# GpSimd multiplies the probabilities of the second and third attention with their reciprocals, and the weave's step lengths follow

## The chip, the cores and the metric

The kernel runs on one core of one Trainium2 chip. What is measured is the device time of one execution in microseconds (us); lower is better. The engines are TensorE (PE, its weight loads PEld), VectorE (DVE), ScalarE (ACT), GpSimd (POOL) and SyncE (SP, which issues most DMAs).

## What is computed

One layer of a decoder trunk on 1024 tokens of width 1024, in float32. One input projection feeds three token mixers: differential attention with 4 heads (A), sliding-window attention with 8 heads, 2 key groups, a window of 128 and sinks (B), and a sparse attention with 8 heads and 2 key groups that adds three branches, compressed, selected and window 512 (C). Their outputs are projected, gated and merged, and an MLP with squared ReLU follows. What the change touches is the normalization in B and C:

```python
# B: softmax over the band with a sink in the denominator
e = jnp.exp(s - m)
p = e / (jnp.sum(e, axis=-1, keepdims=True) + jnp.exp(sk - m))
o = jnp.einsum('bngrqk,bnkgd->bnqgrd', p, vb)
# C: three softmaxes, each weighted by its gate
out = g[..., 0:1] * o_cmp + g[..., 1:2] * o_sel + g[..., 2:3] * o_win
```

With 16 selected blocks of 64 and 1024 tokens, the selected branch sees every causal key.

## The kernel before

Float32 products are split into a high and a low part, and one product is three matmuls, `mm3` (L118 to L120). The split (`split`, L90 and L91) takes an ACT copy for the high part and a subtraction on DVE or POOL for the low one.

Each attention is a sequence of *items*: a pair of 128-query tiles for one head (C, 16 items per key group) or two heads (B, 8 items per key group). An item has *rows* and *groups*. A row issues the logits of one 128-query tile (L711), a minimum on DVE (signs are turned, so it is the maximum; L721, L725, L727, L728, L735, and L1097 for the compressed keys), the exponential with its sum on ACT (L743), and then what the change touches: DVE adds up the sums (L936 to L938 in B, L1042 in C), takes reciprocals (L939; L1043, multiplied by the gates in L1044), and multiplies the probabilities in place: L941 in B (`p`, two heads of up to 256 columns), L1046 in C (`pc`, the 64 compressed columns, then `p` with up to 1024 selected and up to 640 window columns). A group transposes up to four 128x128 blocks of probabilities on PE (L759), splits them out of PSUM into `ph` (ACT, L90) and `pl` (DVE, L91), after POOL zeroed the blocks that are not visible (L756, L757), and later multiplies them with the values into one accumulator (L901, L902). At the end of a head ACT and DVE empty that accumulator (L907, L908); there is one such accumulator, three buffers for logits and two for transposes.

`pipeline` (L670) runs the rows of one item between the groups of the item before it. `step` (L695) emits one group: value products of an earlier group, then the transposes of this one. Each row and step gives two numbers, its PE time and its DVE time as the code estimates them, in us; the second is `d`. `mix` (L155) is the weave: it puts dense work (projections, gates, the first branch product) between these fine steps, as far as the estimated DVE time demands, and what is left over runs behind the last fine step:

```python
for pe, dve in fine:
    now += pe
    goal = max(goal + pace * dve, now - SLACK)
    while step is not None and now < goal and (self.through or ahead < AHEAD):
        now += step
        ahead += 1
        step = next(dense, None)
while step is not None:
    step = next(dense, None)
```

`PACE` (L67) holds the factors: 1.4144 and 1.156 for the two key groups of B, 1.392 and 1.45 for those of C. The dense work is, in B, 64 steps of `project_b` (0.495 each) for the first key group and 32 steps of two gate columns (0.65 each) for the second. In C it is 192 steps of 12 gate columns (`gates`, L1102) for the first key group and `first_branch` (L1148) for the second: 16 and 64 gate steps, 8 branch steps of 2.6 each, then 32 and 16 gate steps and 8 more branch steps. A gate column loads two 128x512 weights, splits them (ACT L90, POOL L91), and stores two results. A branch step loads a weight and a stored gate, runs 12 matmuls, multiplies on DVE (L1162) and stores. Ahead of each key group of C stands `project_c`, which runs alone. `merge_and_mlp` follows C.

PE's order is the order of the program text, so it is this weave. The other engines' order is set when the kernel is built, by a simulated schedule with priorities; each engine then works through its own queue in order.

Of the kernel before, what the change touches and what calls it, by code (L numbers as in the profile page):

```python
# [14 lines left out]
ALU = mybir.AluOpType  # L15
# [60 lines left out]
class Kernel:  # L76
# [835 lines left out]
    def items_b(self, g, sta):  # L912
        nc, at = self.nc, self.at
        bias = self.bias
        for qb, r0 in [(qb, r0) for qb in range(4) for r0 in (0, 2)]:
            pq = [None, None]
            hs = slice(4 * g + r0, 4 * g + r0 + 2)

            def row(j, qb=qb, r0=r0, hs=hs, pq=pq):
                t = 2 * qb + j  # L920
                n = min(2, t + 1) * P
                ps = self.sc()
                p = at.tile([P, 2, 256], F32, name="p", tag=f"p{r0 // 2}", bufs=2)
                l = at.tile([P, 3, 2], F32, name="lb", tag="lb", bufs=4)
                m = at.tile([P, 2], F32, name="mb", tag="mb", bufs=4)
                k0 = max(t - 1, 0)
                d = 0.0
                for i in range(2):
                    self.logits(ps, i * 256, t, sta["logits"][r0 + i], k0 * P, k0 * P + 256)
                for i in range(2):  # L930
                    x = ps[:, i * 256:i * 256 + n]
                    h = 4 * g + r0 + i
                    d += self.near_min(m[:, i:i + 1], x, bias[:, r0 + i, :], self.sink[:, 1, h:h + 1])
                    self.expo(p[:, i, 0:n], x, m[:, i:i + 1], l[:, 0, i:i + 1])

                nc.vector.tensor_tensor(l[:, 1, :], self.sink[:, 0, hs], m, op=ALU.add)  # L936
                nc.scalar.activation(l[:, 1, :], l[:, 1, :], AF.Exp)
                nc.vector.tensor_tensor(l[:, 1, :], l[:, 1, :], l[:, 0, :], op=ALU.add)  # L938
                nc.vector.reciprocal(l[:, 2, :], l[:, 1, :])  # L939
                for i in range(2):  # L940
                    nc.vector.tensor_scalar(p[:, i, 0:n], p[:, i, 0:n], l[:, 2, i:i + 1], None, op0=ALU.mult)  # L941
                pq[j] = (p, k0)
                return 0.43, d + 0.65

            rows = [lambda j=j, row=row: row(j) for j in range(2)]
            groups = []
            kts = list(range(max(2 * qb - 1, 0), 2 * qb + 2))
            box = {}
            for i in range(2):
                def prow(j, kt, i=i, pq=pq):  # L950
                    p, k0 = pq[j]
                    return p[:, i, (kt - k0) * P:(kt - k0 + 1) * P]

                r = r0 + i
                dst = self.od[4 + 2 * g + r // 2, (r % 2) * 64:(r % 2) * 64 + 64, qb * 256:(qb + 1) * 256]
                for grp in ([kts] if len(kts) == 2 else [kts[0:1], kts[1:3]]):
                    def values(i, ph, pl, grp=grp, kts=kts, box=box, dst=dst):
                        kt = grp[i]
                        return self.head_values(box, dst, sta["v"][:, kt, :], ph, pl, kt == kts[0], kt == kts[-1])

                    groups.append(self.group(prow, qb, grp, lambda t, kt: t - 1 <= kt <= t, values))
            yield dict(rows=rows, groups=groups, end=[])

    def items_c(self, g, sta):
        nc, at = self.nc, self.at
        bias4 = self.bias
        for r in range(4):
            for qb in range(4):
# [51 lines left out]
                def win_near(j, mem, qb=qb, r=r, bias=bias, hd=hd, rows=rows):  # L1020
                    t = 2 * qb + j
                    n = (t + 1) * P
                    l, m = mem["l"], mem["m"][:, 2, :]
                    k0 = 0 if t < 4 else t - 1
                    w = n - k0 * P
                    ps = self.sc()
                    cost = self.logits(ps, 0, t, sta["win"][r], k0 * P, k0 * P + max(w, 256))
                    nw = min(w, 256)
                    d, init = 0.0, m[:, 1:2] if k0 else None
                    if w > nw:  # L1030
                        d += self.far_min(m, 1, ps[:, 0:w - nw])
                        init = m[:, 1:2]
                    d += self.near_min(m, ps[:, w - nw:w], bias, 3e38 if init is None else init)
                    p = self.prob(qb, 640, "w")
                    f = 384 if k0 else 0
                    if f:
                        self.expo(p[:, 0:f], mem["wf"], m[:, 0:1], l[:, 1, 1:2])
                    self.expo(p[:, f:f + w], ps[:, 0:w], m[:, 0:1], l[:, 0, 2:3])
                    nw = f + w
                    if "sf" in mem:  # L1040
                        e = 2 if f else 1
                        nc.vector.tensor_tensor(l[:, 0, 1:1 + e], l[:, 0, 1:1 + e], l[:, 1, 0:e], op=ALU.add)  # L1042
                    nc.vector.reciprocal(l[:, 1, 0:3], l[:, 0, 0:3])  # L1043
                    nc.vector.tensor_tensor(l[:, 1, 0:3], l[:, 1, 0:3], self.cgate[:, t, 3 * hd:3 * hd + 3], op=ALU.mult)  # L1044
                    for x, k, i in ((mem["c"], 64, 0), (mem["s"], n, 1), (p, nw, 2)):
                        nc.vector.tensor_scalar(x[:, 0:k], x[:, 0:k], l[:, 1, i:i + 1], None, op0=ALU.mult)  # L1046
                    rows[j] = (mem["c"], mem["s"], p, max(t - 4, 0))
                    return cost, d + 0.55 + 0.52e-3 * (n + nw)

                steps = []  # L1050
                for j in range(2):
# [537 lines left out]
```

## Time and profile before

| | |
|---|---|
| three runs | 2040.56, 2041.63, 2045.64 us, median 2041.63 |
| the profiled execution | 2045.69 us, span 2043.7 us |
| busy over the span | PE 1901.7, PEld 1621.5, DVE 1423.4, ACT 1022.0, POOL 954.3 us |
| second attention | 410 to 562 us of the span |
| third attention, first key group | 612 to 862 us |
| third attention, second key group | 918 to 1196 us |
| granted TensorE clock, mean | 0.980 |

The span runs from the first to the last instruction; the time has some 2 us more around it. A busy time is the union of an engine's instructions. A row of instruction groups names the line, the engine, the operation, what it writes and reads with the shape, how many there were, then their busy time in us, the mean of one in ns, and the idle time in front of them with what ended it. A row of waits reads: who waited, for whom, how long in total, how many times, the longest.

### The profile page before, as it was taken

What the parts mean: (1) busy time and instruction counts of PE and PEld (TensorE: products, weight loads), DVE (VectorE), ACT (ScalarE), POOL (GpSimd) and SP (SyncE); (2) the same over time, 40 slices, a digit from 0 to 9 for tenths busy, and PEclk for the clock granted to TensorE, in tenths of its full rate; (3) what the DMA queues carried; (4) which work ended last, traced back from release to release, by engine and by line L of the source; (5) the groups of instructions that cost most, each with busy time, mean ns of one, the idle gap of its engine ahead of it and who ended that gap; (6) DMA issues with size and microseconds to landing.
All of it is one profiled execution on the core that took longest, in us unless ns stands there. A gap on an engine that the chain in (4) does not pass through costs nothing. (4 is left out here: it accounts for less than half of the span.)

```text
span 2043.7 us, 30701 instructions
## 1 busy us (share of the span) xinstructions
PE 1901.7 (93%) x9838; PEld 1621.5 (79%) x9838; DVE 1423.4 (70%) x3231; ACT 1022.0 (50%) x2626; POOL 954.3 (47%) x1142
## 2 busy tenths in 40 slices
PE   7999888988799999999999899999899998999998
PEld 6888887888688888887888677787688886888876
DVE  6757777788848677648676755657755544889898
ACT  5456556666636555536555533335455544444331
POOL 4455355544352212162222227218444445789784
PEclk9999999999999999999999899999899998999999
DMA  5131022011211111212242456425444446355343
GB/s 218 51 104 52 4 55 59 26 38 37 87 28 61 56 52 51 72 33 91 68 147 77 159 198 204 147 93 161 172 167 160 144 145 247 119 167 163 124 144 114
DMA packets 122558, 219.49 MB, mean 107 GB/s; under 512 B 14420, under 2 KB 35412, under 8 KB 122396
## 3 DMA queue, kind: packets, MB, share of 16 engines
q1 hardware_dynamic: 120812, 211.75, 31.9%
q10 hardware_dynamic: 1584, 5.77, 0.9%
q8 instruction: 78, 1.28, 0.3%
q14 instruction: 84, 0.69, 0.1%
HBM read 156.59 MB, written 64.81 MB: 108 GB/s over the span
## 5 line engine op out<-in xcount | busy, mean ns | idle before, releaser
L91 POOL TENSOR_TENSOR wl<-wr,wh 128x512 fp32r<-128x512 f32 (+3 forms) x246 | 328.8, 1343 | 275.0 <-ACT wh L90 238.8
L90 ACT ACTIVATE wh<-wr 128x512 fp32r<-128x512 f32 (+3 forms) x258 | 150.3, 590 | 183.8 <-PE mm L119 124.1
L711 PE MATMUL sc<-st 128*128 128x256 f32 (+5 forms) x736 | 183.9, 344 | 25.9 <-ACT p L743 25.3
L90 ACT ACTIVATE ph<-tr 128x384 fp32r<-128x384 f32 (+3 forms) x280 | 138.4, 497 | 105.5 <-PE tr L759 87.0
L91 DVE TENSOR_TENSOR pl<-tr,ph 128x384 fp32r<-128x384 f32 (+3 forms) x280 | 155.8, 559 | 40.2 <-ACT ph L90 37.6
L756 POOL MEMSET ph<- 128x128 f32 x152 | 35.7, 235 | 291.3 <-PE ac L901 253.0
L711 PEld LDWEIGHTS sc<-st 128*128 128x128 f32 x736 | 122.8, 192 | 47.5 <-ACT p L743 38.8
L118 PE MATMUL mm<-hh,wh 128*128 128x512 f32 x384 | 158.8, 414 | 0.0
L120 PE MATMUL mm<-hh,wl 128*128 128x512 f32 x384 | 151.5, 395 | 0.0
L119 PE MATMUL mm<-hl,wh 128*128 128x512 f32 x384 | 151.4, 394 | 0.0
L119 PE MATMUL mm<-wl,wh 128*128 128x512 f32 x352 | 139.5, 396 | 9.4 <-POOL wl L91 9.4
L118 PE MATMUL mm<-wh 128*128 128x512 f32 x352 | 139.9, 398 | 8.2 <-DVE x L1471 5.3
L90 ACT ACTIVATE wh<-u 128x512 fp32r<-128x512 f32 x162 | 93.0, 620 | 106.3 <-PE mm L119 27.9
L759 PE MATMUL tr<-ident,p 128*128 128x128 f32 x792 | 129.2, 275 | 16.9 <-ACT o L889 7.8
L120 PE MATMUL mm<-wh,wl 128*128 128x512 f32 x352 | 139.1, 395 | 0.0
L743 ACT ACTIVATE p<-sc,mc 128x256 f32<-128x256 f32 (+5 forms) x200 | 106.7, 538 | 52.0 <-DVE mc L735 47.0
L901 PE MATMUL ac<-ph,st 128*128 128x256 f32 x392 | 109.8, 298 | 19.4 <-DVE ob L908 11.5
L91 POOL TENSOR_TENSOR wl<-s,wh 128x512 fp32r<-128x512 f32 x64 | 89.5, 1405 | 79.3 <-ACT wh L90 79.3
L118 PE MATMUL mm<-wh,hh 128*128 128x384 f32 (+1 forms) x320 | 117.0, 366 | 0.0
L91 DVE TENSOR_TENSOR wl<-u,wh 128x512 fp32r<-128x512 f32 x98 | 112.5, 1150 | 3.9 <-ACT wh L90 3.9
L902 PE MATMUL ac<-pl,st 128*128 128x256 f32 x392 | 106.5, 292 | 6.5 <-DVE pl L91 5.8
L91 POOL TENSOR_TENSOR wl<-u,wh 128x512 fp32r<-128x512 f32 x64 | 98.8, 1557 | 25.1 <-ACT wh L90 25.0
(311 smaller groups left out, 5771.2 us busy)
## 6 DMA issues: line engine op xcount, KB each, us to landing
ud<-u SPq DMA_DIRECT2D x112, 256.0 KB, 2.2
u<-ud SPq DMA_DIRECT2D x98, 256.0 KB, 3.3
wr<-wu SPq DMA_DIRECT2D x76, 256.0 KB, 2.8
wr<-wd SPq DMA_DIRECT2D x64, 256.0 KB, 2.9
gd<-go SPq DMA_DIRECT2D x48, 256.0 KB, 2.0
g<-gd SPq DMA_DIRECT2D x48, 256.0 KB, 3.2
wr<-wg SPq DMA_DIRECT2D x40, 256.0 KB, 2.7
wr<-wbr SPq DMA_DIRECT2D x40, 256.0 KB, 3.0
```

The costliest lines, as they stand in the source:

```text
L90: nc.scalar.activation(hi, src, AF.Copy)
L91: (eng or nc.vector).tensor_tensor(lo, src, hi.bitcast(F32), op=ALU.subtract)
L118: mm(out, lh, rh, start=first, stop=False, skip_group_check=more)
L119: mm(out, lh, rl, start=False, stop=False, skip_group_check=more)
L120: mm(out, ll, rh, start=False, stop=last, skip_group_check=more)
L711: self.nc.tensor.matmul(ps[:, off:off + k1 - k0], q[:, t * P:(t + 1) * P], k[:, k0:k1], start=i == 0, stop=i == 1)
L743: self.nc.scalar.activation(p, ps, AF.Exp, bias=m, scale=-1.0, accum_out=l)
L756: nc.gpsimd.memset(ph[0:rows, o:o + P].bitcast(F32), 0.0)
L759: nc.tensor.transpose(pt[0:rows, o:o + P], src, self.ident)
L901: nc.tensor.matmul(ac, v, ph, start=first, stop=False)
L902: nc.tensor.matmul(ac, v, pl, start=False, stop=last)
```

## The change

The multiplications of L941 and L1046 move from DVE to POOL, with the same operands, and the estimates `d` that those rows hand to the weave become smaller: in B by 0.25 per row (16 rows per key group), in C by 0.52e-3 us for each selected and window column of the row (`n + nw`). `PACE` stays as it is.

```diff
                 nc.vector.tensor_tensor(l[:, 1, :], l[:, 1, :], l[:, 0, :], op=ALU.add)
                 nc.vector.reciprocal(l[:, 2, :], l[:, 1, :])
                 for i in range(2):
-                    nc.vector.tensor_scalar(p[:, i, 0:n], p[:, i, 0:n], l[:, 2, i:i + 1], None, op0=ALU.mult)
+                    nc.gpsimd.tensor_scalar(p[:, i, 0:n], p[:, i, 0:n], l[:, 2, i:i + 1], None, op0=ALU.mult)
                 pq[j] = (p, k0)
-                return 0.43, d + 0.65
+                return 0.43, d + 0.4
...
                     for x, k, i in ((mem["c"], 64, 0), (mem["s"], n, 1), (p, nw, 2)):
-                        nc.vector.tensor_scalar(x[:, 0:k], x[:, 0:k], l[:, 1, i:i + 1], None, op0=ALU.mult)
+                        nc.gpsimd.tensor_scalar(x[:, 0:k], x[:, 0:k], l[:, 1, i:i + 1], None, op0=ALU.mult)
                     rows[j] = (mem["c"], mem["s"], p, max(t - 4, 0))
-                    return cost, d + 0.55 + 0.52e-3 * (n + nw)
+                    return cost, d + 0.55
```

## The prediction

> **What bounds the kernel now.** I read the page's first part, then the stretches in which the edited lines run, then the waits that end in them. Over the whole span TensorE is busy 93%:
>
> ```profile
> PE 1901.7 (93%) x9838; PEld 1621.5 (79%) x9838; DVE 1423.4 (70%) x3231; ACT 1022.0 (50%) x2626; POOL 954.3 (47%) x1142
> ```
>
> The windows view cuts the edited part into stages. Columns: stretch, its length, busy time of PE, PEld, DVE, ACT, POOL, granted clock, DMA share, GB/s.
>
> ```profile
> 410.00:484.00 74.00, 65.01 (x426) 61.08 (x425) 60.26 (x204) 47.44 (x171) 35.98 (x88) 0.95 0.11 30
> 484.00:562.00 78.00, 63.98 (x397) 55.52 (x396) 65.94 (x235) 51.80 (x172) 26.67 (x91) 0.97 0.26 75
> ...
> 612.00:862.00 250.00, 240.70 (x1399) 207.96 (x1398) 182.12 (x603) 147.49 (x427) 55.73 (x109) 1.00 0.18 59
> ...
> 918.00:1118.00 200.00, 191.30 (x1101) 165.05 (x1101) 149.96 (x484) 118.72 (x341) 49.14 (x89) 1.00 0.30 92
> 1118.00:1196.00 78.00, 62.98 (x332) 52.21 (x331) 55.02 (x156) 40.60 (x107) 19.70 (x35) 0.91 0.40 129
> ```
>
> 410 to 562 is the second attention (two key groups), 612 to 862 and 918 to 1196 are the two groups of the third; between them PE runs projections alone. Length minus PE busy is what can be won: 9.0, 14.0, 9.3, 8.7 and 15.0 us, 56.0 in all. The last stretch also lost 0.09 x 78 = 7.0 us to the clock (0.91). So PE's fixed list of work sets the time, DVE is close behind in the second attention (60.26 of 74, 65.94 of 78), and the loss per microsecond is largest from 1118 on. What PE waits for there, and first in the second attention:
>
> ```profile
> PE sc L711 <- ACT p L743: 9.1, 7, 3.2
> PE tr L759 <- DVE pc L1046: 1.8, 1, 1.8
> ```
>
> ```profile
> PE ac L901 <- DVE ob L908: 11.5, 11, 2.0
> ```
>
> The logits wait until ScalarE has read the previous ones, which wait for minima on DVE; the first value product of a head waits until DVE has emptied the only accumulator. Both are DVE latency, bare where no dense matmul stands between. Counting the dense ones alone (first of their three lines) shows why the ends are bad: 6 in the last 24 us of the second attention, 1 in the last 29 of the third.
>
> ```profile
> 538.00:562.00 24.00, 2.57 (x6) 1.42 (x6) 0.90 0.26 78
> ...
> 1167.00:1196.00 29.00, 0.71 (x1) 0.20 (x1) 0.99 0.11 33
> ```
>
> **The change, part by part: DVE.** It loses these groups (columns: busy us, mean ns, idle before):
>
> ```profile
> L1046 DVE TENSOR_SCALAR p<-p,lc 128x640 f32<-128x640 f32 (+7 forms) x128 | 67.8, 571 | 0.0
> ...
> L941 DVE TENSOR_SCALAR p<-p,lb 128x256 f32<-128x256 f32 (+1 forms) x64 | 24.8, 425 | 0.5
> L1046 DVE TENSOR_SCALAR pc<-pc,lc 128x64 f32<-128x64 f32 x64 | 22.2, 346 | 1.7
> L1044 DVE TENSOR_TENSOR lc<-lc,cgate 128x3 f32<-128x3 f32 x64 | 12.8, 200 | 2.0
> ```
>
> That is 24.8 us of 126.2 in the second attention and 67.8 + 22.2 = 90.0 of 387.1 in the third. L1044, which stays, is used below.
>
> **POOL.** It gains 192 + 64 instructions. No multiply by a per-partition scalar ran there, so I bound it:
>
> ```profile
> L91 POOL TENSOR_TENSOR wl<-wr,wh 128x512 fp32r<-128x512 f32 x180 | 258.8, 1441 | 252.6 <-ACT wh L90 233.3 <-DVE lc L1044 15.2 <-PE mm L119 2.4
> ...
> L91 POOL TENSOR_TENSOR st<-raw,st 128x128 fp32r<-128x128 f32 x48 | 23.3, 488 | 22.9 <-ACT st L90 22.9
> ...
> masks.py:199 POOL TENSOR_SCALAR_AFFINE_SELECT ident<-ident 128x128 f32<-128x128 f32 x1 | 0.3, 292 | 0.1
> ```
>
> The two-input rows give (1441 - 488) / 384 = 2.48 ns an element over 171 ns; the one single-input row is 292 ns at 128. The code's sizes add up to 15,360 elements a partition for L941 and 71,680 for L1046 (a head: 64 x 8, selected 4608, window 3840). Upper end, as two inputs: 64 x 0.171 + 38.1 = 49 us and 192 x 0.171 + 177.8 = 211 us. Lower end: what DVE needed, 24.8 and 90.0. I take half the two-input slope through the 292 ns row (133 ns + 1.24 an element), since that row is the nearest in kind: 27.6 and 114 us. POOL is now busy 62.7 us of 152 and 124.6 of 528, so even the upper end leaves it at 73% and 63%: no throughput bound.
>
> **The new waits.** A multiply on POOL waits for L939 or L1044 on DVE, and the transposes of the next item wait for it. Behind it in POOL's queue stand weight residues (L91) and the zeroing of ph and pl; ahead of it can stand a zeroing that itself waits for PE:
>
> ```profile
> POOL ph L756 <- PE ac L901: 101.6, 28, 12.2
> ```
>
> So far that was idle POOL and free (918 to 1196). One row of the third attention, DVE, then POOL, then the transposes that need it:
>
> ```profile
> 707.91 0.16 DVE L1044 TENSOR_TENSOR lc<-lc,cgate 128x3 f32<-128x3 f32 x1
> 708.11 1.30 DVE L1046 TENSOR_SCALAR pc<-pc,lc 128x64 f32<-128x64 f32 x1
> ```
>
> ```profile
> 708.08 1.29 POOL L91 TENSOR_TENSOR wl<-wr,wh 128x512 fp32r<-128x512 f32 x1 [5.99 <-DVE lc L1044]
> ```
>
> ```profile
> 712.68 0.38 PE L759 MATMUL tr<-ident,pc 128*128 128x128 f32 x2
> ```
>
> The multiply ended at 709.41, 3.27 us before its use. On POOL, behind the same 1.29 us residue, it would end near 709.37 + 0.21: hidden, also at 0.33 (upper end). Of all these multiplies one made PE wait, the 1.8 us of the waits quoted above; I add that and nearly as much again for late rows, 3 us. The ends: 0, and a mean multiply (114 / 192 = 0.6 us) in each of 32 items, 19 us.
>
> The same rows show DVE and POOL blocking each other: the 64-element multiply took 1.30 us beside a residue against a mean of 346 ns. That contention leaves with the edit, but L1044 and its like (two inputs from SBUF) have it too: 0.16 us alone, 200 ns on average, with POOL at 24% of the third attention. At (124.6 + 114) / 528 = 45% I take another 0.04 us on each such instruction (L728 56, L1042 40, L1044 64, L936 and L938 32 each: 224): 9 us, so DVE still sheds 106. Upper bound, each meeting a multiply as often as POOL is busy and waiting out its whole mean of 0.6 us: 224 x 0.45 x 0.6 = 60 us.
>
> The Trainium skill (SBUF — State Buffer, "Who interferes with whom") states that a VectorE instruction with two SBUF inputs contends with a GpSimd one that reads SBUF, and that the later one blocks fully; by that rule the edit swaps one blocked instruction for another, and the sum would be that of the second rival below. The 1.30 us row agrees in kind.
>
> **The weave.** `mix` puts dense steps in until pace x the sum of the figures d is reached. The code's figures for one group of the third attention sum to 159.9 over 194 fine steps; the edit takes 0.52e-3 x 8448 x 4 = 17.6 off. First group: 1.392 x 159.9 - 99.8 (its own PE figures) = 122.8 of 124.8 dense before; 1.392 x 142.3 - 99.8 = 98.3 after, so about 40 of 192 steps are pushed behind the last fine one. Second group, also 124.8 of dense work: 1.45 x 159.9 - 99.8 = 132.1 used it up 18 fine steps early (the empty 29 us); 1.45 x 142.3 - 99.8 = 106.6 reaches the end and leaves 6 branch steps of 2.6 behind it. Second attention (0.25 x 16 = 4.0 off 41.3 and off 44.0): in its first half 1.4144 x 37.3 - 25.9 = 26.9 of 31.7, so 9 of 64 steps stay behind; in its second, stepped through by the same rule, the last dense step moves from the 39th fine step to the 50th of 50. What these weigh on PE:
>
> ```profile
> 1118.17 0.39 PE L118 MATMUL mm<-xh,wh 128*128 128x512 f32 x1
> ...
> 1118.86 0.39 PE L118 MATMUL mm<-xh,wh 128*128 128x512 f32 x1
> ...
> 1120.89 0.28 PE L901 MATMUL ac<-ph,st 128*128 128x256 f32 x1
> ```
>
> A dense step is 0.69 us, a branch step 2.72; so 27.6 + 16.3 + 9 x 0.53 = 48.7 us of dense work leaves the fine stretches and runs alone behind them. That costs nothing if those stretches, 96% PE in the third attention, get as much shorter. Each of the 6 branch steps takes along its weight load, its gate load and its store (256 KB each) on SP's queue, one ScalarE and one POOL split and one DVE product; the merge's loads stand behind them on SP, under 16.3 us of PE work. I price that at 0; at worst PE waits for its first two loads, some 5 us.
>
> **The sum**, against this execution's 2045.69 us. 410 to 484: 9.0 lost, DVE a fifth lighter but thinner cover, -2. 484 to 562: 14.0 lost, the end now covered, -5. First group, -2 of 9.3, second to 1118, -1 of 8.7: PE-bound already. From 1118: 22.0 lost with the clock; the 56 us of work would lose 2.5 at the rate of the stretch before; I credit half of the 19.5 between, since coarse steps and a bare drain of the last item remain, -10. Late rows +3. Sum -17, 2028.7. The median of the runs is 4.06 us below this execution, so 2024.6, said as 2025.
>
> **Rivals.** *The fine stretches don't get shorter* (the other side). They may be held by the chain minimum, exponential, sum, multiply, transpose, and not by PE's list; ScalarE is at 59% in the first group and would rise to 66%. Then the 48.7 us run on top. The place is 612 to 862; it decides where more than 17 / 48.7 = 35% is not made up. For it: PE waits for ACT p and DVE ob are latency; against: 240.70 of 250 busy. At 60% kept on top: 2024.6 + 29 = 2054.
>
> *The port eats it.* With the 60 us bound DVE sheds 55 of 115, the gains of 20 halve, and late rows stay: -10 + 3 gives 2035; with the 19 us of late rows instead of 3, 2051. For it: the 1.30 us row; against: L1044's mean of 200 ns beside a POOL at 24%.
>
> *DVE was the bound in the second attention after all*, and the end of the third closes well: 14 of the 23.0 us there, 19 of 22.0 from 1118, 4 in between, no late row: 2041.6 - 37 = 2005.
>
> *The edit is hidden*: PE's list stays the bound and its few gaps keep their length, 2042.
>
> **How the numbers follow.** Forecast 0.42 (own range 2014 to 2033), DVE-bound 0.16, port with the nearer price 0.08 and with the further 0.06, hidden 0.06, stretches don't shorten 0.22. Within 0.3% (6.1 us, about what a measurement here tells from no change) is 2035.5 to 2047.8: hidden 0.06, half of the nearer port 0.04, and edges of the neighbours 0.06, together 0.16. Faster: 0.42 + 0.16 + 0.04, less 0.03 for the forecast's edge, 0.59. Slower: 0.22 + 0.06 less 0.03, 0.25. The range reaches to the outer cases, 2005 to 2056.
>
> **What the profile after would show.** No L941 or L1046 on DVE, 256 multiplies on POOL of 28 and 114 us; DVE some 100 us lighter. Dense steps until the end of each attention, some 28 us of gates alone after the first group and 16 us of branch steps after the second. PE's idle share in the last 80 us before the merge falls from 19% to below 12%. Wrong would make me: transposes L759 waiting for POOL L1046, L1042 or L728 above 400 ns, a first group whose fine stretch stays near 250 us, or multiplies above 2 us.

## The result, and the profile after

The changed kernel is slower. Its median is 2061.3 us (five runs, 2053.0 to 2065.9) against 2040.56 us before on the same chip (2039.7 to 2045.6), a ratio of 1.0087 with a 95% interval of 1.0064 to 1.0110. The interval is about 9 us wide, and the medians differ by 20.7 us where that ratio makes 18; differences below are between medians, so a few us of them mean little. The forecast was 2025, its range 2005 to 2056: even the range missed. The profiled execution took 2065.94 us, its span is 2064.2 us and its mean clock 0.972, where the one before had 2045.69, 2043.7 and 0.980; both are some 5 us above their medians.

The first part of the page after:

```profile
PE 1909.1 (92%) x9838; PEld 1628.0 (79%) x9838; DVE 1343.6 (65%) x2975; ACT 1022.4 (50%) x2626; POOL 1226.0 (59%) x1398
```

DVE is 79.8 us lighter (1423.4 before), POOL 271.7 us heavier (954.3). PE issues as many matmuls as before and is busy 7.4 us longer, at a lower mean granted clock. The windows of the kernel after, cut where its own stages end (columns as in the prediction):

```profile
406.00:484.00 78.00, 70.64 (x475) 65.87 (x474) 57.04 (x198) 54.07 (x194) 64.05 (x127) 0.98 0.15 42
484.00:561.00 77.00, 64.82 (x365) 56.54 (x365) 53.42 (x182) 47.42 (x155) 53.55 (x119) 0.87 0.22 65
608.00:854.00 246.00, 228.80 (x1339) 199.09 (x1338) 151.69 (x516) 145.09 (x425) 159.92 (x207) 0.97 0.16 51
854.00:878.00 24.00, 24.00 (x107) 19.87 (x106) 2.13 (x3) 4.89 (x9) 4.93 (x4) 1.00 0.28 91
878.00:933.00 55.00, 51.89 (x234) 40.78 (x232) 19.39 (x37) 17.94 (x47) 30.85 (x43) 0.94 0.14 38
933.00:1160.00 227.00, 212.94 (x1236) 183.87 (x1235) 151.04 (x500) 140.84 (x409) 154.12 (x193) 0.99 0.25 82
1160.00:1199.00 39.00, 31.82 (x161) 26.53 (x160) 21.28 (x42) 20.27 (x43) 25.23 (x29) 0.82 0.64 191
1199.00:1221.00 22.00, 11.82 (x51) 9.52 (x50) 4.84 (x8) 2.19 (x5) 1.29 (x1) 0.83 0.81 280
```

Four things stand in these rows. The fine stretch of the third attention's first group (third row) lost dense work and yet has more idle PE: 246.00 - 228.80 = 17.2 us against 10.2 before (258.00 - 247.78, in the windows of the kernel before under e11). The gates pulled out of it run alone at 100% (fourth row). `project_c` for the second group (fifth row) takes 54.5 us by its first and last matmul where it took 47.2. And in the last row, the branch steps behind the last fine step, PE works 11.8 of 22 us. Measured by the first and last matmul of each stage, the 20.5 us between the two spans are: -1.9 up to the end of the first `project_c` (1.4 of it by 384 us, ahead of any edited line), +11.8 in the first group with its gates alone, +7.3 in the second `project_c`, +7.7 in the second group with its branch steps alone, and -4.4 from the merge on.

The groups of POOL in the kernel after, shapes apart, from 400 to 1222 us:

```profile
L1046 POOL TENSOR_SCALAR p<-p,lc 128x640 f32<-128x640 f32 x40 | 75.4, 1889 | 0.0
L941 POOL TENSOR_SCALAR p<-p,lb 128x256 f32<-128x256 f32 x56 | 52.0, 941 | 10.6 <-DVE lb L939 5.7 <-ACT ph L90 3.5 <-ACT st L562 1.2
L1046 POOL TENSOR_SCALAR pc<-pc,lc 128x64 f32<-128x64 f32 x64 | 29.8, 466 | 84.2 <-DVE lc L1044 75.5 <-ACT ph L90 4.3 <-PE sc L711 1.8
...
L1046 POOL TENSOR_SCALAR p<-p,lc 128x1024 f32<-128x1024 f32 x8 | 22.8, 2848 | 0.0
```

From 640 to 1024 columns the time grows by 959 ns: 2.50 ns an element over some 0.29 us. The idle column tells the order: POOL stands idle 84.2 us ahead of the first multiply of a row (`pc`), 75.5 of it for L1044, and not at all ahead of the other two. The three come as one burst. What PE waits for in the same stretch:

```profile
PE ac L901 <- DVE ob L908: 15.6, 18, 3.0
PE ac L901 <- POOL ph L756: 12.8, 9, 3.7
PE mm L118 <- DVE g L1162: 10.2, 1, 10.2
...
PE tr L759 <- POOL p L1046: 1.5, 4, 0.6
PE ac L901 <- POOL pl L757: 1.2, 1, 1.2
```

The second row is new. The transposes hardly wait for the multiplies (fourth row shown); the value products wait for the *zeroing* of `ph`, a memset of 0.2 us that stands behind the multiplies in POOL's queue. One such case in the timeline of the kernel after:

```profile
834.67 0.16 DVE L1044 TENSOR_TENSOR lc<-lc,cgate 128x3 f32<-128x3 f32 x1
...
835.00 0.45 POOL L1046 TENSOR_SCALAR pc<-pc,lc 128x64 f32<-128x64 f32 x1 [2.08 <-DVE lc L1044]
...
835.42 4.71 POOL L1046 TENSOR_SCALAR p<-p,lc 128x1024 f32<-128x1024 f32 x2
...
835.79 0.28 PE L901 MATMUL ac<-ph,st 128*128 128x256 f32 x1
...
840.07 0.21 POOL L756 MEMSET ph<- 128x128 f32 x1
...
840.33 0.58 PE L901 MATMUL ac<-ph,st 128*128 128x256 f32 x1 [3.69 <-POOL ph L756]
```

POOL waits 2.08 us for the reciprocals, then works 5.1 us through a row whose probabilities PE needs later, and only then zeroes the block that PE needs now. PE is idle 3.69 us and comes back at half clock: this matmul takes 0.58 us, its like 0.28 before the gap.

The 10.2 us wait stands at the end of the branch steps. DVE in the timeline of the kernel after:

```profile
1204.76 0.69 DVE L1162 SCALAR_TENSOR_TENSOR g<-g,mm 128x512 f32<-128x512 f32 x1 [1.48 <-DMA g<-gd]
1212.13 0.69 DVE L1162 SCALAR_TENSOR_TENSOR g<-g,mm 128x512 f32<-128x512 f32 x1 [6.68 <-DMA y<-yd]
1219.29 0.69 DVE L1162 SCALAR_TENSOR_TENSOR g<-g,mm 128x512 f32<-128x512 f32 x1 [3.23 <-DMA g<-gd]
```

And PE in the same timeline, at the end of its last branch step and the start of the merge:

```profile
1209.56 0.39 PE L120 MATMUL mm<-xh,wl 128*128 128x512 f32 x1
1220.12 0.76 PE L118 MATMUL mm<-ob,wh 128*128 128x512 f32 x1 [10.18 <-DVE g L1162]
```

PE is done with the branch steps at 1209.9, but their last products with the gates come 7 us apart: a gate is loaded into one of two buffers, multiplied in place and stored from it, and only then can the next load start, behind the merge's loads on SP. The result of a branch step stays in PSUM until its product has read it, and the merge's first matmul waits for the last of these products: the 10.18 us. With fine steps between the branch steps this ring had time; alone, at 2.7 us of PE work each, they do not.

### The profile page after: what moved, and what is told of

It reads as the page before. It is cut to its first block, busy times and chain, and to the rows that moved or that the text cites. A ratio compares the mean times of both kernels' runs of the same rounds, so it can differ in the third digit from the quotient of the medians.

```text
span 2064.2 us, 30762 instructions
## 1 busy us (share of the span) xinstructions
PE 1909.1 (92%) x9838; PEld 1628.0 (79%) x9838; DVE 1343.6 (65%) x2975; ACT 1022.4 (50%) x2626; POOL 1226.0 (59%) x1398
## 5 line engine op out<-in xcount | busy, mean ns | idle before, releaser
L1046 POOL TENSOR_SCALAR p<-p,lc 128x640 f32<-128x640 f32 (+7 forms) x128 | 204.8, 1613 | 0.0
L711 PE MATMUL sc<-st 128*128 128x256 f32 (+5 forms) x736 | 182.5, 342 | 19.7 <-ACT p L743 19.3
L118 PE MATMUL mm<-hh,wh 128*128 128x512 f32 x384 | 161.1, 420 | 0.0
L759 PE MATMUL tr<-ident,p 128*128 128x128 f32 x792 | 135.3, 284 | 20.0 <-ACT o L889 8.6
L120 PE MATMUL mm<-hh,wl 128*128 128x512 f32 x384 | 153.0, 398 | 0.0
L118 PE MATMUL mm<-wh 128*128 128x512 f32 x352 | 140.5, 399 | 8.7 <-DVE x L1471 5.0
L901 PE MATMUL ac<-ph,st 128*128 128x256 f32 x392 | 112.8, 305 | 33.0 <-POOL ph L756 12.8
L120 PE MATMUL mm<-wh,wl 128*128 128x512 f32 x352 | 139.4, 396 | 0.0
L743 ACT ACTIVATE p<-sc,mc 128x256 f32<-128x256 f32 (+5 forms) x200 | 107.2, 540 | 64.9 <-DVE mc L735 64.2
L118 PE MATMUL mm<-wh,hh 128*128 128x384 f32 (+1 forms) x320 | 117.0, 366 | 0.0
L759 PEld LDWEIGHTS tr<-ident,p 128*128 128x128 f32 x792 | 95.6, 145 | 26.7 <-ACT o L889 11.0
```

What stands on the lines that cost most here:

```text
L118: mm(out, lh, rh, start=first, stop=False, skip_group_check=more)
L120: mm(out, ll, rh, start=False, stop=last, skip_group_check=more)
L711: self.nc.tensor.matmul(ps[:, off:off + k1 - k0], q[:, t * P:(t + 1) * P], k[:, k0:k1], start=i == 0, stop=i == 1)
L743: self.nc.scalar.activation(p, ps, AF.Exp, bias=m, scale=-1.0, accum_out=l)
L759: nc.tensor.transpose(pt[0:rows, o:o + P], src, self.ident)
L901: nc.tensor.matmul(ac, v, ph, start=first, stop=False)
```

## The experiments

Two theories were set against each other. *The burst* (theory Q, later B, in the expectations): POOL's multiplies are in the way of the zeroing, so the loss comes with the move. *The lengths* (theory W): the dense work pulled out of the fine stretches is not made up, and its seams cost, so the loss comes with `d`. A third, *the total* (theory T), holds that POOL's 291 us of multiplies are too many wherever they stand. Each kernel's ratio is against the kernel before in the same group, whose medians were 2038.4 to 2040.4 us. `project_c(1)` in the expectations is the second `project_c`.

**e1: the multiplies alone**, with the old lengths, so that PE's order is that of before.

```diff
-                return 0.43, d + 0.4
+                return 0.43, d + 0.65
-                    return cost, d + 0.55
+                    return cost, d + 0.55 + 0.52e-3 * (n + nw)
```

> Only the engine of the multiplies is changed (POOL); the step lengths are those of before, so PE's order is that of before. Theory Q (queue): the multiplies, 0.29 us + 2.5 ns an element in the trace after, hold up the zeroing of ph and pl behind them on POOL, PE waits for it (12.8 us of such waits in the third attention after), the weave has little to do with it: 2052, slower by 8 to 14 us, with those waits as large as after. Theory W (weave): the loss is made where the dense work that was pulled out runs alone, at project_c(1) and at the merge; with the old lengths there is none of it, and DVE's relief shows: 2030, faster by 5 to 15 us.

Measured: 2063.4 us, ratio 1.0113 (1.0093 to 1.0134). The move alone is as slow as the whole change. PE's waits in e1, 401 to 1210 us:

```profile
PE ac L901 <- DVE ob L908: 18.8, 16, 3.0
PE ac L901 <- POOL ph L756: 16.3, 11, 3.7
...
PE ac L902 <- POOL pl L757: 7.2, 4, 3.9
```

16.3 + 7.2 = 23.5 us for the zeroing. That this is about the loss of 23.0 is partly chance: some waits are shorter than before, and part of the loss is the same matmuls running slower (below, under e11).

**e2: the lengths alone**, with the multiplies on DVE (the diff of the change without its two `gpsimd` lines).

> Only the step lengths are changed; the multiplies stay on DVE. PE's order is that of the changed kernel. Theory Q: the lengths cost little: 2044, within 6 us of before. Theory W: the fine stretches have less cover, DVE is as loaded as before, and the seams at project_c(1) (54.5 us after against 47.2 before) and at the merge (PE waits 10.2 us after) come back in full: 2058, slower by 14 to 22 us.

Measured: 2058.36 us, 1.0095 (1.0073 to 1.0116). The lengths alone cost 18 us as well. The second `project_c` takes 53.6 us, and PE waits 11.1 us for L1162, as after. By stages, against before: +8.1 us up to the end of the gates that run alone behind the first group, +6.5 in the second `project_c`, +10.6 up to the merge, and -8.3 behind it. The two halves do not add: 23.0 + 18.0 = 41, together 20.7.

**e3: the whole change in the second attention only.**

> The whole change in the second attention alone (multiply on POOL and shorter lengths there); the third is as before. After, the second attention ended 1.9 us earlier than before, so both theories expect 2038 to 2044 here. Were it slower by more than 6 us, the loss would begin in the second attention and only show later.

Measured: 2038.53 us, 0.9994 (0.9977 to 1.0010): nothing. All of the loss is in the third attention.

**e4: the change, with the zeroing on DVE.** This takes the small work out of the queue in which the multiplies stand.

```diff
-    nc.gpsimd.memset(ph[0:rows, o:o + P].bitcast(F32), 0.0)
+    nc.vector.memset(ph[0:rows, o:o + P].bitcast(F32), 0.0)
```

(and the same for `pl`)

> The changed kernel, with the zeroing of ph and pl (152 pairs) moved from POOL to DVE, at some 0.2 us each. PE's order is that of the changed kernel. Theory Q: nothing that PE waits for stands behind the multiplies any more, the 12.8 us of waits on POOL ph are gone: 2046 to 2050, that is 11 to 15 us under the changed kernel. Theory W: the seams stay, 2056 to 2061.

Measured: 2042.33 us, 1.0011 (0.9998 to 1.0025). Of the 20.7 us, 18.8 are gone (2042.33 - 2040.4 = 1.9 are left). Multiplies, lengths and POOL's 291 us are still there. The transposes now wait 7.7 us for the multiplies (5.0 for L1046 `p`, 2.7 for `pc`), which after they did for 1.5.

**e5: e1, with the zeroing on DVE.**

> Multiplies on POOL, zeroing of ph and pl on DVE, step lengths of before (PE's order is that of before). By now the multiplies alone cost 23 us and the lengths alone 18, and zeroing on DVE took 19 off the changed kernel. If both causes are separate (multiplies hold up the zeroing; pulled-out dense work stumbles at two seams), both are absent here and DVE's relief is left: 2026, faster by 10 to 18 us, project_c(1) at 47 to 49 us, no PE wait of 10 us at the merge. If the zeroing was only the cover of a general lateness of POOL, PE waits for POOL p and pc (7.7 us in the kernel with zeroing on DVE) grow instead: 2038 to 2045.

Measured: 2038.21 us, 0.9990 (0.9978 to 1.0002), 25 us under e1, but the kernel is not faster than before. The time is that of the second expectation, its reason is not: PE's waits for the multiplies did not grow against the 7.7 us of e4. They are 4.3 + 1.0 + 0.9 = 6.2 us in e5:

```profile
PE tr L759 <- POOL p L1046: 4.3, 4, 1.9
...
PE tr L759 <- POOL p L941: 1.0, 1, 1.0
...
PE tr L759 <- POOL pc L1046: 0.9, 1, 0.9
```

**e6 and e7: the seams.** Branch steps write their product to a buffer of its own, so that the gate's buffer is free after the product and not after the store; and `project_c` takes its first four weights into the other set of buffers, which the last gates do not hold.

```diff
-                nc.vector.scalar_tensor_tensor(g, g, 1.0, ps, ...)
-                nc.sync.dma_start(self.yd[d, :, s], g)
+                y = self.rp.tile([P, 512], F32, name="yo", tag="raw", bufs=2)
+                nc.vector.scalar_tensor_tensor(y, g, 1.0, ps, ...)
+                nc.sync.dma_start(self.yd[d, :, s], y)
...
-   tag="x" if k >= self.w_bufs else "w"
+   tag="x" if (k < self.w_bufs if n == 512 else k >= self.w_bufs) else "w"
```

e6 is the change with these edits:

> The changed kernel with its lengths and its zeroing on POOL, and two edits of the seams: the branch product goes into a buffer of its own, so that the next gate load need not wait for the store; and project_c takes its first four weights into the buffers that the gates don't use. If the seams are what the lengths cost: project_c(1) from 54.5 to about 48 us, the 10.2 us wait of PE at the merge below 4, together 2048, 11 to 14 us under the changed kernel, with the 12.8 us of PE waits on POOL ph still there. If the lengths cost in the fine stretches instead: 2058 to 2062.

e7 is e4 with them:

> The changed kernel with the zeroing on DVE and both seam edits: everything of the change, without its two side effects. If they are the two causes: 2042 less 12 to 16, 2028, below before and near the kernel with the old lengths. If the thinner cover itself costs: 2038 to 2042.

Measured: e6 2052.53 us, 1.0063 (1.0048 to 1.0079); e7 2041.17 us, 1.0004 (0.9987 to 1.0020). Both seams close: the second `project_c` is back at 47.1 and 47.2 us, and the wait in front of the merge falls to 2.6 us (waits of e6):

```profile
PE mm L118 <- DVE yo L1163: 2.6, 1, 2.6
```

Yet on the time they are worth some 7 us in one pair (20.7 against 13.3 us over before; the intervals of the two ratios overlap) and nothing that can be told in the other (1.9 against 2.0). e7 thus came out where it was expected if the thinner cover itself costs. Part of the reason is behind the seam. The first stretches after the merge starts, in e4, which waits 9.7 us in front of it, and then in e7:

```profile
1198.30:1238.30 40.00, 39.96 (x170) 33.00 (x171) 12.71 (x18) 7.79 (x13) 23.27 (x18) 0.96 0.69 217
1238.30:1298.30 60.00, 58.65 (x258) 47.85 (x257) 50.20 (x54) 24.75 (x44) 41.03 (x27) 1.00 0.66 207
```

```profile
1185.80:1225.80 40.00, 38.79 (x161) 31.26 (x162) 11.23 (x16) 8.11 (x13) 18.46 (x14) 0.96 0.75 252
1225.80:1285.80 60.00, 54.60 (x230) 43.84 (x229) 37.66 (x47) 20.54 (x36) 38.98 (x28) 0.97 0.59 182
```

After a late start the merge runs without gaps, since the loads went on during the wait; after an early one it waits for them. From its first matmul to the end e4 takes 837.8 us, e7 849.2 (before: 848.5, after: 844.1). The same holds in all profiles: 837.8 to 844.1 us in the four kernels with a wait of some 10 us in front of the merge (after, e2, e4, e9), 848 to 853 in the other ten. That wait was thus mostly a wait moved forward.

**e8: a control, the kernel before with the zeroing on DVE.**

> Control: the kernel before, with the zeroing on DVE. PE's order is that of before. DVE gains some 304 x 0.2 = 60 us of work over the attentions and POOL loses 70; nothing else. If the gain of the kernels with zeroing on DVE comes from the multiplies' new place and not from the zeroing itself: 2040 to 2052, not faster. If ACT's waits on POOL's zeroing mattered before already: 2030 to 2036.

Measured: 2040.32 us, 1.0007 (0.9993 to 1.0021). The zeroing on DVE gains nothing of itself; what it gains over the changed kernel and e1, in e4 and e5, is what the multiplies had spoilt.

**e9: the change, with L1046 multiplying by a constant.** This leaves out the normalization of the third attention; the multiplies have their sizes, but wait for no reciprocal.

```diff
-   nc.gpsimd.tensor_scalar(x[:, 0:k], x[:, 0:k], l[:, 1, i:i + 1], None, op0=ALU.mult)
+   nc.gpsimd.tensor_scalar(x[:, 0:k], x[:, 0:k], 0.5, None, op0=ALU.mult)
```

> The changed kernel with the third attention's multiplies on POOL by the constant 0.5 and not by the row's reciprocal, which leaves that normalization out. It prices the multiply itself. If the per-partition scalar is what costs 2.5 ns an element: 640 columns in 0.7 to 1.0 us against 1.89 us after, and a time of 2045 to 2052. If any such pass costs that on POOL: 1.6 to 1.9 us, and 2055 to 2065.

Measured, in one run: 2032.9 us, beside 2038.43 before, and below both expectations. The multiply costs nearly the same (groups of POOL in e9):

```profile
L1046 POOL TENSOR_SCALAR p<-p 128x640 f32<-128x640 f32 x40 | 72.4, 1812 | 20.8 <-ACT p L743 20.0 <-DVE ob L91 0.5
```

1812 ns against 1889: the operand from memory is not what makes it slow. But now the idle column is not empty: each multiply waits for its own exponential (ACT, L743), the burst is broken up, and PE waits only 0.8 us for `ph` from L756. POOL's multiplies are nearly as long in all (277 us against 291), which speaks against *the total*.

**e10: the kernel before without the multiplies** of L941 and L1046 (both normalizations are left out), old lengths.

> The kernel before without the multiplies (the probabilities of the second and third attention stay unnormalized), step lengths and PE's order of before, zeroing on POOL. It is the whole relief of DVE, 115 us, at no price anywhere. If DVE's load had set PE's gaps, as the prediction's sum took it: 2020 or below (its gains added to 20 us). If PE's gaps are latency and the weave's own (the kernel with the multiplies on POOL and the zeroing on DVE came out level): 2034 to 2041.

Measured: 2016.59 us, 0.9889 (0.9871 to 0.9907). 22 us is what it is worth to leave the multiplies out: DVE's relief, and also the multiply's own time between the reciprocals and the transposes. The run does not part the two.

**e11: e1, but each branch is multiplied as soon as its own sum is there.** `pc`, the selected and the window columns take a reciprocal each, right behind their exponentials, in place of one for all three at the end of the row. Zeroing on POOL, old lengths, the same 192 multiplies.

```diff
...
+    def scaled(self, x, k, l, i, far, t, hd):
+        if far:
+            nc.vector.tensor_tensor(l[:, 0, i:i + 1], l[:, 0, i:i + 1], l[:, 1, i - 1:i], op=ALU.add)
+        c = self.cgate[:, t, 3 * hd + i:3 * hd + i + 1]
+        nc.vector.reciprocal(l[:, 2, i:i + 1], l[:, 0, i:i + 1])
+        nc.vector.tensor_tensor(l[:, 2, i:i + 1], l[:, 2, i:i + 1], c, op=ALU.mult)
+        nc.gpsimd.tensor_scalar(x[:, 0:k], x[:, 0:k], l[:, 2, i:i + 1], None, op0=ALU.mult)
...
```

> Multiplies on POOL with the step lengths of before, zeroing on POOL, but in the third attention each branch takes its own reciprocal and is multiplied as soon as its exponential is done, where the changed kernel multiplies all three at the row's end in one burst (0.45 + 2.2 + 1.9 us at 64, 768 and 640 columns). DVE gets about 5 more small instructions a row, some 50 us. Theory B (burst): what holds up the zeroing is the burst, not POOL's total; the waits on POOL ph fall from 16.3 us (move only) to under 4, and with part of DVE's relief left: 2030, 5 to 15 us under before. Theory T (total): POOL's 235 us of multiplies hold the zeroing up wherever they stand: 2050 to 2062.

Measured: 2031.56 us, 0.9965 (0.9951 to 0.9978): 32 us under e1, and faster than both kernels. Groups of POOL in e11, the multiplies of all sizes but `pc`:

```profile
L1094 POOL TENSOR_SCALAR p<-p,lc 128x640 f32<-128x640 f32 (+7 forms) x128 | 206.2, 1617 | 74.7 <-DVE lc L1093 42.5 <-ACT p L743 10.7 <-ACT ph L90 10.6
```

After, the same group was 204.8 us with no idle time in front. PE's wait in e11:

```profile
PE ac L901 <- POOL ph L756: 0.5, 1, 0.5
```

And the row of 1024 columns on POOL in e11, to be read against the burst at 835 above:

```profile
835.99 2.85 POOL L1094 TENSOR_SCALAR p<-p,lc 128x1024 f32<-128x1024 f32 x1 [1.97 <-ACT pc L743]
838.78 0.21 POOL L756 MEMSET ph<- 128x128 f32 x1
838.93 0.21 POOL L757 MEMSET pl<- 128x128 f32 x1
839.10 0.45 POOL L1094 TENSOR_SCALAR pc<-pc,lc 128x64 f32<-128x64 f32 x1
840.61 1.89 POOL L1094 TENSOR_SCALAR p<-p,lc 128x640 f32<-128x640 f32 x1 [1.05 <-DVE lc L1093]
```

Same work, but the zeroing now stands between two multiplies. Before, e1 and e11 have the same order on PE, so their stages compare one to one; they are cut at their own matmuls, and the stretches of each group hold the same number of matmuls within one. First group, the second `project_c`, second group, first of the kernel before, then e1, then e11:

```profile
610.30:868.30 258.00, 247.78 (x1444) 213.96 (x1443) 187.18 (x613) 152.69 (x437) 57.72 (x116) 1.00 0.19 59
868.10:915.70 47.60, 47.60 (x235) 39.10 (x234) 19.79 (x39) 15.82 (x45) 29.54 (x42) 1.00 0.09 29
915.70:1194.30 278.60, 255.80 (x1443) 218.59 (x1440) 206.81 (x642) 160.91 (x452) 70.65 (x126) 0.98 0.33 103
```

```profile
601.20:866.10 264.90, 249.99 (x1443) 216.01 (x1442) 155.74 (x516) 152.50 (x436) 165.96 (x212) 0.99 0.18 57
865.90:914.70 48.80, 48.25 (x234) 39.00 (x233) 19.90 (x39) 16.30 (x45) 29.60 (x42) 1.00 0.09 27
914.70:1209.00 294.30, 262.69 (x1443) 225.55 (x1441) 175.87 (x546) 160.79 (x452) 181.18 (x222) 0.94 0.31 97
```

```profile
602.20:854.60 252.40, 246.77 (x1444) 214.09 (x1442) 170.76 (x661) 152.32 (x436) 166.20 (x211) 1.00 0.19 60
854.40:901.90 47.50, 47.50 (x235) 39.02 (x233) 18.76 (x39) 15.93 (x44) 29.51 (x42) 1.00 0.11 31
901.90:1173.70 271.80, 252.94 (x1443) 217.42 (x1441) 188.11 (x690) 159.94 (x452) 181.47 (x222) 0.99 0.33 105
```

POOL is as busy in e11 as in e1 (166.20 and 165.96; 181.47 and 181.18). e1 loses 6.9 and 15.7 us in the two groups against before, e11 gains 5.6 and 6.8. In the second group of e1, 8.8 us of the loss are more idle PE, and 6.9 us are the same 1443 matmuls taking longer (262.69 against 255.80), at a granted clock of 0.94 against 0.98; in e11 it is 0.99.

**e12: e11 with the new lengths and both seam edits.**

> The same with the step lengths of the change and both seam edits (own buffer of the branch product, project_c's first weights in the free buffers). Theory B: 2024 to 2034, as the constant-scalar kernel (2033 with both seams open) less 12 for the seams, plus the small instructions. Theory T: 2045 to 2053, as the changed kernel with the seams closed (2052.5).

Measured: 2033.7 us, 0.9978 (0.9963 to 0.9994). With the burst gone and the seams closed, the new lengths add nothing to e11 (2.1 us more, within the spread).

What follows: the burst is shown, in two ways: by taking the zeroing out from behind it (e4, e5, with e8 as the control) and by breaking it up (e9, in one run, and e11), of which e11 leaves the zeroing and all of the work on POOL. The seams of the lengths are shown in the traces, and e2 shows that the lengths cost 18 us with the multiplies on DVE. How much of those 18 us each seam holds is not settled: the edits that close both were not run on e2, and gave some 7 us and nothing where they were run. In no pair of kernels in which PE hardly waits for the zeroing did the lengths gain anything: before to e2, e5 to e4 and e7, e11 to e12.

## Why the prediction was wrong

**The step that failed: "The new waits".** It named what was to go wrong ("Behind it in POOL's queue stand ... the zeroing of ph and pl") and then priced only one of the two waits, that of the transposes for the multiplies. That price came out by luck: 3 us forecast, 1.5 measured, but only because PE already stood waiting for the zeroing; with that out of the way it is 7.7 us in e4 and 6.2 in e5. The zeroing got no price. It cost 12.8 + 1.5 = 14.3 us of waits for `ph` and `pl` in the profile after and 23.5 in e1, and taking it out of POOL's queue was worth 18.8 (after to e4) and 25 us (e1 to e5). The quoted row of POOL's zeroing, 101.6 us in which it waited for PE, should have been the warning: the zeroing of a block is released by PE and needed by PE soon after, so it has little slack, and anything long ahead of it is paid by PE. I read it only in the other direction, as what the multiplies might stand behind.

**POOL's price was mis-sized.** I took 1.24 ns an element from the one single-input row at hand, 27.6 and 114 us; measured 56.8 (L941) and 234.6 us (L1046: 204.8 and 29.8), above even my upper ends of 49 and 211. The slope is the 2.48 ns of the two-input rows, the intercept larger. The sum of the work was harmless, as the prediction said: POOL is at 65% of the first group's fine stretch (159.92 of 246). It mattered because it doubled the length of each burst: 4.7 us for 1024 + 640 columns, 2.3 at the price that I took.

**The pulled-out work was priced at 0, "at worst ... 5 us".** The weave's arithmetic was right: the dense work reached the end of each attention, 24 us of gates ran alone (forecast 28), and four branch steps were left behind the second group (forecast 6). The work that left was not all made up in the fine stretches (below, under the rivals), and the cover failed in two places I had not priced: the second `project_c` (+7.3 us) and the ring of two gate buffers (10.2 us, twice the worst case, of which 4.4 came back behind the merge). I had listed the gate loads and stores and SP's queue, but not counted the ring's turn: load, product, store, load.

**The gains of 20 did not come as summed.** e10 gets 22 us, but that is not the same 20. 15 of the sum's were to come from dense work that covers the two ends, through the new lengths, and e10 has the old ones. The cover itself worked where nothing else went wrong: PE's idle share of the last 80 us before the merge is 18.5% in e5 and 13.4% in e7, 17.5% in e11 and 12.8% in e12. But the time did not fall with it: e7 is 3.0 us over e5, e12 2.1 over e11. So against 3 us of new waits stood gains that, with the multiplies in bursts on POOL, were not there: e5, where nothing waits for the zeroing and the lengths are old, gains 1 us. Its first group is 6.4 us shorter than before (251.6 against 258.0 us; e11 gains 5.6 and e10 6.6 there), its second group is no shorter (278.6 both; e11 gains 6.8 and e10 11.4). Part of the 7 us between e5 and e11 is the transposes' wait for the multiplies, 6.2 us in e5 and 1.2 in e11 (all waits of PE for `p` and `pc`). The rest, and why e11 keeps only 7 of e10's 22, stays open.

**Contention was smaller than forecast.** DVE was to shed 106 of 114.8 us and sheds 79.8. Most of what is missing is not contention: e10, without any of these multiplies, sheds only 94.8 (1328.6 busy), since busy times of neighbouring instructions overlap and do not add (in the trace before, DVE's busy time without them is 1325.2). Of the other 15 us, the five rows that the prediction priced at 9 hold 5.0 (46.4 us in e10, 51.4 after; 48.0 before). L728 went from 209 to 326 ns, L1044 from 200 to 198. The Trainium skill (SBUF — State Buffer, "Who interferes with whom") says that a VectorE instruction with two SBUF inputs contends with a GpSimd one that reads SBUF. The 326 ns agree in kind. The 198 ns do not speak against it: in the profile after, 16 of the 64 runs of L1044 meet a POOL instruction other than a memset and take 313 ns, the other 48 take 160; for L728 it is 41 of 56, with 388 and 155 ns, while the reciprocal (L1043, one input) takes 175 either way. The mean cost of a meeting, 0.15 and 0.23 us, is far below the length of a multiply, 1.6 us on the mean for `p`. (The 1.30 us row that the prediction sets beside this rule is a multiply with one tensor input, so it is not a case of two.) The rival "The port eats it" falls: its sign, L728 above 400 ns, did not come, and DVE shed 79.8 us where that rival had 55.

**The second attention** was to gain 7 us; e3 shows nothing (0.9994). The dense steps did move to its end as computed, but in the profile after its second half runs at a clock of 0.87.

**The rivals.** "The fine stretches don't get shorter" had the sign, the place and nearly the time (2054 against 2061): 24.3 us of gates came out of the first group's fine stretch, which shrank by 12.7 (257.2 to 244.5), so 48% was not made up, beyond the 35% at which it was to decide. That figure mixes two effects. The move alone made the stretch 6.9 us longer (before to e1), and that was the burst in front of the zeroing: where the zeroing does not stand behind one (e5, e10, e11), the stretch is 5.6 to 6.6 us shorter than before. The lengths alone made it shorter by 19.7 us (e1 to after), 16.4 (before to e2), 12.8 (e5 to e4), 14.4 (e5 to e7) and 18.7 (e11 to e12). So with waits for the zeroing or without them, 19 to 47% of the 24.3 us were not made up, and to that extent the rival was right. Whether the softmax chain that it blamed holds the stretch was not tested.

**Signs named beforehand.** "Multiplies above 2 us" came (2.85) and "a first group whose fine stretch stays near 250" came (244.5); the transposes waiting for L1046 did not (1.5 us). The idle share of the last 80 us before the merge was to fall from 19% below 12%; it rose to 22% (62.25 of 80 us busy from 1140 to 1220).

## What to carry to other kernels

Before work is moved to an engine with room, list what else stands in its queue, and ask of each small instruction who releases it, who waits for it, and how long the new work ahead of it runs without a break; a low busy share answers none of this. If the work must move, cut it so that each piece is issued when its own input is ready: here the kernel came out 23 us slower with the third attention's multiplies in bursts of three, and 7 us faster with the same ones issued one by one. And work that is hidden among other steps is not free once it runs alone: count the turn of each ring of buffers that it uses against its bare pace.

## What the runs showed of the hardware

A multiply by a per-partition scalar on POOL took 2.50 ns an element in float32, no less than the two-input subtraction beside it (2.48), and a constant in place of the scalar saved 4% (1812 against 1889 ns at 640 columns). I had expected half.

PE gaps cost twice. After the idle 3.69 us at 840 a matmul took 0.58 us instead of 0.28, and shorter gaps did the same: in the kernel before, PE was idle for 2.55 us up to 1134.01, and the 128x512 matmuls of L118 to L120 took 0.63 us behind it and 0.39 in front. The granted clock of the second group fell to 0.94 in e1 where it was 0.98 before and 0.99 in e11, which has the same matmuls on PE in the same order.

A DVE instruction with two inputs from SBUF took 155 to 160 ns when no POOL instruction but a memset ran at its start (L728 and L1044 in the profile after), and 313 to 388 ns on the mean when one did.
